# Output projection: every second weight tile's low half made by a negative on ScalarE and an adding transfer issued by GpSimd

## The chip, the cores and the metric

The kernel runs on one core of a Trainium2 chip. The metric is device time in microseconds of one execution; lower is better.

## What is computed

One layer of a streaming encoder, for 256 tokens of width 4096, all in 32-bit floats. It is cut here to what matters for the change, which lies in the last two lines but one:

```
proj = einsum('bsd,dc->bsc', x, w_in)              # one wide input projection
fox_out  = forgetting attention of some columns    # 16 heads of 128
rwkv_out = RWKV-7 scan of other columns            # 32 heads of 64
h    = concatenate([fox_out, rwkv_out], -1) * silu(z)
out  = einsum('bsc,cd->bsd', h, w_out)             # 4096 x 4096: the output projection
x    = layernorm(ALPHA * x + out, ln_gain, ln_bias)
```

## The kernel before

**Products in two halves.** TensorE's fast 32-bit format (F32R) keeps fewer bits than a float. So each operand is split into a high half, which is the value cast to F32R, and a low half, which is the value minus the high half. A product is then three matmuls into the same PSUM tile: high by high, low of the activations by high of the weights, and high of the activations by low of the weights. In the output projection these are the three lines of `project` (L882, L883, L884); L884 is the only one that reads the low half of the weights.

**The weight stream.** All weights are read once, in tiles of 128 partitions by 1024 values (512 KB), two steps of the contraction by 512 output columns. `stream` lists them in the order of use, first the input projection (names such as w3_1_7), then the output projection: `wo{b}_{q}` is tile q (0 to 15) of the block b (0 to 7) of 512 output columns. The profile leaves b out: all blocks' tiles 9 are wo_9, with wo_9h and wo_9l for their halves. Two functions keep the stream ahead of TensorE:

- `load` lets SP start the transfer of the next tile into one of four raw buffers (tag "wr").
- `fetch` takes the oldest raw tile and calls `split`: ScalarE casts it into one of four buffers for high halves (tag "wh", L141), VectorE subtracts the high half from the raw tile into one of three buffers for low halves (tag "wl", L142).

`weights(name)` is called ahead of each tile's matmuls and fetches until three tiles are ready. The order on each engine's queue comes from a scheduler, which starts from the order in which the program is written; an instruction waits on semaphores for what it reads and for the release of the buffer that it writes. A low half therefore waits for the last matmul that read the low half three tiles back, a high half for the last one that read the high half four tiles back, and a load for the last reader of the raw tile four back.

**The blocks.** Blocks 0 and 1 overlap with the end of the scan and with a change of memory pools. Blocks 2 to 7 run one after the other: for each of 16 tiles, two steps j and two halves m of the tokens, three matmuls each, 12 matmuls of 128x512 to a tile. After each block, VectorE adds the result to the residual and takes statistics (`add`, `gain`). In block 7, four tiles are held in buffers of their own (`kept`), and the second half of the tokens of the last tiles comes late, beside the layer norm.

Of the kernel before, what the change touches and what calls it, by code (L numbers as in the profile page):

```python
# [10 lines left out]
F32 = mybir.dt.float32  # L11
BF16 = mybir.dt.bfloat16
F32R = mybir.dt.float32r
AF = mybir.ActivationFunctionType
ALU = mybir.AluOpType
AX = mybir.AxisListType

P = 128
S = 256
D = 4096  # L20
KT = D // P
# [25 lines left out]
NB = D // OB  # L47
# [37 lines left out]
def layer(ctx: ExitStack, tc: tile.TileContext, xt, xtok, w_main, w_lora, w_first, muv, w_o, up, par, mulora, fbias, lng, lnb, cst, out):  # L85
    nc = tc.nc
# [5 lines left out]
    wpool = ctx.enter_context(tc.tile_pool(name="wpool", bufs=3))  # L92
# [20 lines left out]
    for n, (k0, k1) in enumerate(pieces):  # L113
        raw = spool.tile([P, 2 * S], F32, tag="xr", name=f"xr{n}", bufs=4)
        nc.sync.dma_start(out=raw[:, : (k1 - k0) * S], in_=xt[:, k0:k1, :].rearrange("p k t -> p (k t)"))
        x_raw.append(raw)
        raw = spool.tile([P, 2 * LA], F32, tag="lr", name=f"lr{n}", bufs=4)
        (nc.scalar if n < 3 else nc.sync).dma_start(out=raw[:, : (k1 - k0) * LA], in_=w_lora[:, k0:k1, :].rearrange("p k c -> p (k c)"))
        l_raw.append(raw)
        raw = wpool.tile([P, 1024], F32, tag="wr", name=f"wr{n}", bufs=4)  # L120
# [17 lines left out]
    def split(src, n, name, pool=wpool, tag="", cols=1024):  # L138
        hi = pool.tile([P, cols], F32R, tag="wh" + tag, name=name + "h", bufs=4 if pool is wpool else 1)
        lo = pool.tile([P, cols], F32R, tag="wl" + tag, name=name + "l")  # L140
        nc.scalar.copy(hi[:, :n], src[:, :n])  # L141
        latest[0] = nc.vector.tensor_tensor(lo[:, :n], src[:, :n], hi[:, :n].bitcast(F32), ALU.subtract)  # L142
        return hi, lo
# [14 lines left out]
    for n, (k0, k1) in enumerate(pieces):  # L158
# [6 lines left out]
        hi, lo = split(l_raw[n], (k1 - k0) * LA, f"wl{n}", spool, str(n % 3), 2 * LA)  # L165
        for j, m in steps(k1 - k0, False):
            mm(acc_l[m], m, k0 + j, hi, lo, j * LA, LA)
        hi, lo = split(w_raw[n], (k1 - k0) * LB, f"wr{n}")
# [38 lines left out]
    stream += [(f"wo{b}_{q}", w_o[b][:, 2 * q : 2 * q + 2, :]) for b, q in outs]  # L207
    stream.reverse()
    kept = {f"wo{NB - 1}_{KT // 2 - LATE + n}": n for n in range(LATE - 3)}
    rpool = None  # L210
    ready = []
    raws = []

    def load():
        if stream:
            name, src = stream.pop()
            raw = wpool.tile([P, 1024], F32, tag="wr", name=name, bufs=4)
            nc.sync.dma_start(out=raw, in_=src.rearrange("p k c -> p (k c)"))
            raws.append((name, raw))

    def fetch():
        while len(raws) < 3 and stream:
            load()
        if raws:
            name, raw = raws.pop(0)
            if name not in kept:
                ready.append((name, *split(raw, 1024, name)))
                return
            hl = []
            for j in range(4):  # L230
                hl.append(xpool.tile([P, OB], F32R, tag=f"x{4 * kept[name] + j}", name=f"{name}_{j}"))
            for j in range(2):
                r = raw[:, j * OB : (j + 1) * OB]
                nc.scalar.copy(hl[j], r)
                nc.vector.tensor_tensor(hl[2 + j], r, hl[j].bitcast(F32), ALU.subtract)
            ready.append((name, hl[:2], hl[2:]))

    def weights(name):
        while len(ready) < 3 and (stream or raws):
            fetch()  # L240
        got, hi, lo = ready.pop(0)
        assert got == name
        return hi, lo
# [704 lines left out]
    for b, q in outs:  # L948
        if q == 0:
            pool, tag = (ps, "ps") if b == 1 or b and b % 2 == 0 else (pp, "pp")  # L950
            oacc[b] = [pool.tile([P, 512], F32, tag=tag, name=f"oacc{b}_{m}") for m in range(2)]
        acc = oacc[b]
        hi, lo = weights(f"wo{b}_{q}")
        for j in range(2):
            k = 2 * q + j
# [46 lines left out]
    def moments(m):  # L1002
        mv = rpool.tile([P, 2], F32, name=f"mv{m}")
        sd = rpool.tile([P, 1], F32, name=f"sd{m}")
        rs = rpool.tile([P, 1], F32, name=f"rs{m}")
        s2 = rpool.tile([P, 1], F32, name=f"s2{m}")
        zh = rpool.tile([P, 1], F32R, name=f"zh{m}")
        z = factors(m, "d")
        nc.gpsimd.memset(z[:, 3:5], 1.0)
        za = factors(m, "a") if m else None  # L1010
        add(m, NB - 1)
        nc.vector.bn_aggr(mv, sums if m else st[m].rearrange("p b s -> p (b s)"))
        mean = mv[:, 0:1]
        nc.scalar.activation(sd, mv[:, 1:2], AF.Sqrt, bias=lneps)
        nc.vector.reciprocal(rs, sd)
        nc.vector.tensor_tensor(s2, mean, rs, ALU.mult)
        nc.vector.tensor_copy(zh, s2)
        nc.vector.tensor_copy(z[:, 0:3:2], zh.bitcast(F32).to_broadcast([P, 2]))
        last = nc.vector.tensor_tensor(z[:, 1:2], s2, zh.bitcast(F32), ALU.subtract)
        s2s.append(s2)  # L1020
        if m:
            for n, (v, at) in enumerate(((mean, (slice(0, 3, 2), slice(1, 2))), (sd, (slice(3, 5), slice(5, 6))))):
                h = rpool.tile([P, 1], F32R, name=f"zah{n}")
                nc.scalar.copy(h, v)
                nc.scalar.copy(za[:, at[0]], h.bitcast(F32).to_broadcast([P, 2]))
                nc.scalar.activation(za[:, at[1]], h.bitcast(F32), AF.Identity, scale=-1.0, bias=v)
        rss.append(rs)
        return z, za, last.ins
# [18 lines left out]
    z0, _, last = moments(0)  # L1047
# [26 lines left out]
    for n in range(HALVED):  # L1074
        b = HALVED + n
# [62 lines left out]
```

## Time and profile before

| | |
|---|---|
| median of 3 runs | 1917.95 us (1917.94 to 1918.83) |
| the profiled execution | 1917.13 us, its span 1915.3 us |
| TensorE busy | 1903.0 us, 99% of the span |
| VectorE, ScalarE, GpSimd busy | 1398.3, 985.9 and 261.5 us |
| granted TensorE clock, mean | 0.999 |
| blocks 2 to 6 of the output projection | about 1639 to 1859 us in the span |

PE stands for TensorE's matmuls, PEld for its weight loads, DVE for VectorE, ACT for ScalarE, POOL for GpSimd and SP for SyncE. The span goes from the first to the last instruction; the time of an execution has some 2 us more around it. A row of the timeline has the start and the duration in us, the engine, the line, the operation and what it writes and reads, and in brackets how long the engine had been idle before it and what ended that. Matmuls overlap: one is shown with 0.39 us, and the next starts about 0.23 us after it.

### The profile page before, as it was taken

The page shows a single profiled execution, that of the slowest core. Times are in us where ns is not written, and L with a number is a line of the kernel's source. Part 1 is how long each engine was busy: PE and PEld are TensorE (multiplying, and loading weights), DVE is VectorE, ACT ScalarE, POOL GpSimd, SP SyncE. Part 2 cuts the span into 40 slices and gives each one's busy share as a digit, 9 for nine tenths or more (in the row PEclk, how much of TensorE's full clock was granted, in tenths as well). Part 3 has the DMA queues.
Part 4 walks back from the last instruction along what each step waited for, and adds up shares of the span by engine and source line. Part 5 has one row for each costly group of instructions (what it writes and reads, how often), then busy time and mean ns, then how long its engine had stood idle before and what let it go on. Part 6 is the DMA issues. An engine that isn't in the chain of part 4 may idle for free.

```text
span 1915.3 us, 27998 instructions
## 1 busy us (share of the span) xinstructions
PE 1903.0 (99%) x9784; PEld 1584.8 (83%) x9784; DVE 1398.3 (73%) x2359; ACT 985.9 (51%) x1543; POOL 261.5 (14%) x463
## 2 busy tenths in 40 slices
PE   9999999999999999999999999999999999999998
PEld 9878888888888888888888888888888878888886
DVE  6677868786877687768776877787778865765555
ACT  6554565455545654465446554645464554444332
POOL 0022102110211021102200220022002201000000
PEclk9999999999999999999999999999999999999999
DMA  9578767876787677767876687668767976876664
GB/s 338 152 232 230 205 198 235 229 216 190 228 232 220 189 228 224 230 191 217 233 227 193 208 242 226 194 208 246 215 196 207 300 255 199 271 222 202 183 203 170
DMA packets 269682, 420.58 MB, mean 220 GB/s; under 512 B 142370, under 2 KB 169396, under 8 KB 269540
## 3 DMA queue, kind: packets, MB, share of 16 engines
q1 hardware_dynamic: 269108, 418.10, 72.8%
q8 instruction: 77, 1.26, 0.3%
q10 hardware_dynamic: 432, 0.69, 0.1%
q14 instruction: 65, 0.53, 0.1%
HBM read 389.07 MB, written 29.64 MB: 219 GB/s over the span
## 4 chain that ended last, share of the span: by engine, by line
PE 97%; DVE 1%; ACT 0%; issue 0%; DMA 0%; DVEq 0%; ACTq 0%
PE acc L147 24%; PE acc L149 24%; PE acc L148 24%; PE oacc L884 6%; PE oacc L882 6%; PE oacc L883 6%; PE rh L648 1%; PE gp L534 1%; PE up L679 1%; PE sp L689 1%; PE accl L147 1%; PE accl L148 1%; PE accl L149 1%; PE yp L711 0%; PE yp L709 0%; PE fsp L746 0%
## 5 line engine op out<-in xcount | busy, mean ns | idle before, releaser
L761 POOL COPY pT<-lg 32x96 f32<-32x96 f32 x128 | 58.5, 457 | 641.7 <-DVE lg L757 636.9
L604 DVE TENSOR_REDUCE xc<-prod 128x8 f32<-128x16 f32 (+30 forms) x248 | 72.7, 293 | 6.5
L571 POOL COPY BKt<-BK 32x192 f32<-32x192 f32 x128 | 68.6, 536 | 58.6 <-DVE BK L568 53.6
L601 DVE TENSOR_TENSOR prod<-Nb,xc 128x8 f32<-128x8 f32 (+30 forms) x248 | 72.2, 291 | 3.0
L142 DVE TENSOR_TENSOR w_0l<-w,w_0h 128x1024 fp32r<-128x1024 f32 x31 | 38.7, 1248 | 38.2 <-ACT w_0h L141 25.0
L141 ACT CAST w_0h<-w 128x1024 fp32r<-128x1024 f32 x31 | 32.5, 1048 | 51.5 <-DMA w<-in_w_main_dram 31.0
L142 DVE TENSOR_TENSOR w_11l<-w,w_11h 128x1024 fp32r<-128x1024 f32 x31 | 37.9, 1224 | 23.3 <-PE acc L149 17.7
L142 DVE TENSOR_TENSOR w_9l<-w,w_9h 128x1024 fp32r<-128x1024 f32 x31 | 38.0, 1225 | 21.6 <-issue 8.0
L142 DVE TENSOR_TENSOR w_10l<-w,w_10h 128x1024 fp32r<-128x1024 f32 x31 | 38.0, 1224 | 20.6 <-ACT w_10h L141 8.0
L142 DVE TENSOR_TENSOR w_15l<-w,w_15h 128x1024 fp32r<-128x1024 f32 x31 | 38.0, 1226 | 19.4 <-issue 15.9
L141 ACT CAST w_8h<-w 128x1024 fp32r<-128x1024 f32 x31 | 32.6, 1052 | 37.6 <-DMA w<-in_w_main_dram 12.5
L141 ACT CAST w_1h<-w 128x1024 fp32r<-128x1024 f32 x31 | 32.7, 1054 | 34.8 <-DMA w<-in_w_main_dram 18.9
L142 DVE TENSOR_TENSOR w_6l<-w,w_6h 128x1024 fp32r<-128x1024 f32 x31 | 37.9, 1221 | 17.3 <-ACT hry L722 10.3
L147 PE MATMUL acc<-w_15h,x 128*128 128x512 f32 x124 | 50.2, 405 | 0.0
L147 PE MATMUL acc<-w_9h,x 128*128 128x512 f32 x124 | 50.0, 403 | 0.0
L141 ACT CAST w_6h<-w 128x1024 fp32r<-128x1024 f32 x31 | 32.6, 1053 | 33.0 <-PE acc L148 23.0
L147 PE MATMUL acc<-w_14h,x 128*128 128x512 f32 x124 | 49.5, 399 | 0.0
L141 ACT CAST w_13h<-w 128x1024 fp32r<-128x1024 f32 x31 | 32.5, 1050 | 32.6 <-PE acc L148 31.9
L147 PE MATMUL acc<-w_1h,x 128*128 128x512 f32 x124 | 49.1, 396 | 0.0
L147 PE MATMUL acc<-w_2h,x 128*128 128x512 f32 x124 | 49.1, 396 | 0.0
L147 PE MATMUL acc<-w_0h,x 128*128 128x512 f32 x124 | 49.1, 396 | 0.0
L147 PE MATMUL acc<-w_5h,x 128*128 128x512 f32 x124 | 49.1, 396 | 0.0
(818 smaller groups left out, 6633.7 us busy)
## 6 DMA issues: line engine op xcount, KB each, us to landing
w<-in_w_main_dram SPq DMA_DIRECT2D x496, 512.0 KB, 4.1
wo<-in_w_o_dram SPq DMA_DIRECT2D x128, 512.0 KB, 4.1
bt<-bk SPq DMA_DIRECT2D x88, 128.0 KB, 4.2
Nb<-nd SPq DMA_DIRECT2D x16, 512.0 KB, 4.6
hd<-hl SPq DMA_DIRECT2D x29, 256.0 KB, 2.2
h<-hd SPq DMA_DIRECT2D x29, 256.0 KB, 6.1
wr<-in_w_first_dram SPq DMA_DIRECT2D x15, 384.0 KB, 6.1
lr<-in_w_lora_dram SPq DMA_DIRECT2D x14, 336.0 KB, 6.5
```

Source lines behind the costliest of these rows:

```text
L141: nc.scalar.copy(hi[:, :n], src[:, :n])
L142: latest[0] = nc.vector.tensor_tensor(lo[:, :n], src[:, :n], hi[:, :n].bitcast(F32), ALU.subtract)
L147: nc.tensor.matmul(acc[:, :n], xs[k][:, 0, tt], hi[:, o : o + n], start=(k == 0), stop=False)
L148: nc.tensor.matmul(acc[:, :n], xs[k][:, 1, tt], hi[:, o : o + n], start=False, stop=False)
L149: nc.tensor.matmul(acc[:, :n], xs[k][:, 0, tt], lo[:, o : o + n], start=False, stop=(k == KT - 1))
L571: nc.gpsimd.tensor_copy(BKt[B * b : B * (b + 1), :, :, B * a : B * (a + 1)], BK[B * a : B * (a + 1), :, : NCH - 1, B * b : B * (b + 1)])
L601: first = nc.vector.tensor_tensor(prod[:, :, :, s + 1 :], nb[:, :, s : s + 1, s + 1 :].to_broadcast([P, 2, NJ, w]), xc[:, :, :, s + 1 :], ...
L604: solved = nc.vector.tensor_reduce(xc[:, :, :, s : s + 1], prod[:, :, :, s:], AX.X, ALU.add)
L761: (nc.gpsimd.tensor_copy if b % 2 else nc.scalar.copy)(pT[B * b : B * (b + 1), :, B * a : B * (a + 1)], lg[B * a : B * (a + 1), :, B * b : ...
L882: nc.tensor.matmul(acc, ht[k][:, 0, tt], hi, start=(k == 0), stop=False)
L883: nc.tensor.matmul(acc, ht[k][:, 1, tt], hi, start=False, stop=False)
L884: nc.tensor.matmul(acc, ht[k][:, 0, tt], lo, start=False, stop=(k == KT - 1))
```

## The change

For the tiles 1, 3, 5, ... 15 of the blocks 2 to 6 (40 of the 80 tiles there) the low half is no longer a subtraction on VectorE. ScalarE casts the raw tile as before, then writes the negative of the high half into the low half's buffer, and GpSimd issues a transfer that reads the same weights from memory a second time and adds them to that buffer. The sum, weights minus high half, is the same low half. The buffers and their numbers stay as they are, and so do all the other tiles.

```diff
+    summed = {f"wo{b}_{q}" for b in range(2, NB - 1) for q in range(1, KT // 2, 2)}
...
-            raws.append((name, raw))
+            raws.append((name, raw, src))
...
-            name, raw = raws.pop(0)
+            name, raw, src = raws.pop(0)
+            if name in summed:
+                hi = wpool.tile([P, 1024], F32R, tag="wh", name=name + "h", bufs=4)
+                lo = wpool.tile([P, 1024], F32R, tag="wl", name=name + "l")
+                nc.scalar.copy(hi, raw)
+                nc.scalar.mul(lo, hi.bitcast(F32), -1.0)
+                nc.gpsimd.dma_start(out=lo, in_=src.rearrange("p k c -> p (k c)"), accum_op=ALU.add)
+                ready.append((name, hi, lo))
+                return
```

Nine lines are added ahead of most of the program, so that a line number after is larger by 9 for most rows: L884 of before is L893 after. The cast of a summed tile is L230, its negative L231, its transfer L232.

The scheduler places these as follows. On VectorE in block 3, tiles 8 to 12, before:

```order
L142 TENSOR_TENSOR wo_8l<-wo_8_16279,wo_8h 128x1024
L142 TENSOR_TENSOR wo_9l<-wo_9_16297,wo_9h 128x1024
L142 TENSOR_TENSOR wo_10l<-wo_10_16315,wo_10h 128x1024
L142 TENSOR_TENSOR wo_11l<-wo_11_16333,wo_11h 128x1024
L142 TENSOR_TENSOR wo_12l<-wo_12_16351,wo_12h 128x1024
```

After, with the statistics of the block before standing ahead of them:

```order
L142 TENSOR_TENSOR wo_4l<-wo_4_16204,wo_4h 128x1024
L142 TENSOR_TENSOR wo_6l<-wo_6_16241,wo_6h 128x1024
L882 TENSOR_SCALAR rt_17525<-rh_17523,cs 6x512
L883 SCALAR_TENSOR_TENSOR rows<-rr_17520,cs,rt_17525 6x512
L142 TENSOR_TENSOR wo_8l<-wo_8_16290,wo_8h 128x1024
L142 TENSOR_TENSOR wo_10l<-wo_10_16327,wo_10h 128x1024
L142 TENSOR_TENSOR wo_12l<-wo_12_16364,wo_12h 128x1024
```

The odd tiles' subtractions are gone and nothing has taken their place. ScalarE's queue at the same place, and GpSimd's, stand in the prediction. On TensorE four matmuls around the first tiles of blocks 2 to 4 change places with their neighbours; else its order is the same.

## The prediction

> **What bounds the kernel now.** I read the page first, for the busiest engine and for the chain of work that ended last.
>
> ```profile
> span 1915.3 us, 27998 instructions
> PE 1903.0 (99%) x9784; PEld 1584.8 (83%) x9784; DVE 1398.3 (73%) x2359; ACT 985.9 (51%) x1543; POOL 261.5 (14%) x463
> ...
> PE 97%; DVE 1%; ACT 0%; issue 0%; DMA 0%; DVEq 0%; ACTq 0%
> ```
>
> TensorE is busy for 99% of the span, and 97% of the chain is its matmuls. An average says little about one stage, so next the windows, one for each of the five blocks that the change touches.
>
> ```profile
> core 0: us, PE busy (x) PEld busy (x) DVE busy (x) ACT busy (x) POOL busy (x), PEclk, DMA share, GB/s
> 1639.00:1683.00 44.00, 43.97 (x194) 36.07 (x193) 30.50 (x35) 20.44 (x23) 0.00 (x0) 1.00 0.85 277
> ...
> 1771.00:1815.00 44.00, 44.00 (x195) 36.43 (x195) 23.67 (x24) 17.07 (x17) 0.00 (x0) 1.00 0.65 201
> 1815.00:1859.00 44.00, 44.00 (x195) 36.41 (x194) 23.66 (x24) 16.89 (x16) 0.00 (x0) 1.00 0.64 195
> sum 220.00, PE 219.97 PEld 181.79 DVE 128.50 ACT 91.12 POOL 0.00; mean PE 43.99 PEld 36.36 DVE 25.70 ACT 18.23 POOL 0.00
> ```
>
> TensorE is busy for 219.97 of 220.00 us at the full granted clock (1.00). VectorE, from which the change takes work, is busy for 128.50 us, ScalarE for 91.12 us, GpSimd not at all. The DMA engines are at 0.64 to 0.85 of their time. The waits of the weight loads into TensorE in 1640 to 1890 us have one row, and it is all that VectorE costs TensorE there.
>
> ```profile
> PEld oacc L884 <- DVE wo_2l L142: 0.5, 1, 0.5
> ```
>
> So a lighter VectorE is worth 0.5 us at most. What decides is whether the low half of a weight tile, made the new way, is still there when TensorE asks for it. The timeline of block 3 shows how early it is now. L882 and L883 multiply by the high half, L884 by the low half.
>
> ```profile
> 1699.40 1.05 ACT L141 CAST wo_9h<-wo 128x1024 fp32r<-128x1024 f32 x1 [1.10 <-PE oacc L883]
> ...
> 1701.92 0.39 PE L884 MATMUL oacc<-wo_6l,h 128*128 128x512 f32 x1
> ...
> 1702.12 1.06 ACT L141 CAST wo_10h<-wo 128x1024 fp32r<-128x1024 f32 x1 [1.67 <-PE oacc L883]
> 1702.15 0.39 PE L882 MATMUL oacc<-wo_7h,h 128*128 128x512 f32 x1
> ...
> 1702.41 1.23 DVE L142 TENSOR_TENSOR wo_9l<-wo,wo_9h 128x1024 fp32r<-128x1024 f32 x1 [1.55 <-PE oacc L884]
> ...
> 1704.87 0.39 PE L882 MATMUL oacc<-wo_8h,h 128*128 128x512 f32 x1
> ...
> 1707.59 0.39 PE L882 MATMUL oacc<-wo_9h,h 128*128 128x512 f32 x1
> ...
> 1707.82 0.19 PEld L884 LDWEIGHTS oacc<-wo_9l,h 128*128 128x128 f32 x1
> ```
>
> One tile takes TensorE 1704.87 - 1702.15 = 2.72 us. There are three buffers for low halves, so wo_9l can only be written when TensorE has let go of wo_6l: the subtraction starts at 1702.41, ends at 1703.64, and the first weight load that goes with wo_9l stands at 1707.82. That is 4.18 us in hand. A waiting matmul would hold up everything behind it on TensorE, whose queue is in order here.
>
> **Removed.** 40 of the 80 subtractions (8 in each of 5 blocks), 1.23 us each, 49 us of VectorE. TensorE never waited for them but in the row above, so they return between 0 and 0.5 us; I take 0. ScalarE's cast of the high half stays as it is. The raw tile of a summed name becomes free after that cast, not after the subtraction, so SP may send the load four tiles on a little sooner. No load is late now (the casts of block 3 above start on "PE oacc L883"), so that also gives nothing.
>
> **Added on ScalarE.** 40 negatives of 128x1024. The nearest row is its cast of the same shape, 1.06 us. With two casts to a pair of tiles that is 3 x 1.06 = 3.2 us in 5.44 us: ScalarE has the room. But the place in its queue counts. ScalarE in block 3, before:
>
> ```order
> L141 CAST wo_8h<-wo_8_16279 128x1024
> L141 CAST wo_9h<-wo_9_16297 128x1024
> L141 CAST wo_10h<-wo_10_16315 128x1024
> L141 CAST wo_11h<-wo_11_16333 128x1024
> L141 CAST wo_12h<-wo_12_16351 128x1024
> ```
>
> And the same place after (L230 is the cast of a summed tile, L231 the negative):
>
> ```order
> L141 CAST wo_8h<-wo_8_16290 128x1024
> L231 ACTIVATE wo_7l<-wo_7h 128x1024
> L230 CAST wo_9h<-wo_9_16308 128x1024
> L141 CAST wo_10h<-wo_10_16327 128x1024
> L231 ACTIVATE wo_9l<-wo_9h 128x1024
> L230 CAST wo_11h<-wo_11_16345 128x1024
> L141 CAST wo_12h<-wo_12_16364 128x1024
> ```
>
> All 40 negatives stand behind the cast of the next tile. That cast (wo_10h) waits for the end of wo_6h on TensorE, the same moment at which the buffer of wo_9l comes free. So the negative doesn't start at 1702.41 but after 1702.12 + 1.06 = 1703.18, and ends at about 1704.25 (1.06 again). From there to 1707.82 are 3.57 us, and the whole transfer has to fit in them: the hand-over to GpSimd, its issue, the data, the signal back.
>
> **Added on GpSimd and the DMA engines.** 40 transfers of 512 KB that read the weights once more and add them to what stands in the buffer. GpSimd's queue holds nothing else in these blocks:
>
> ```order
> L1018 MEMSET zd_17841 128x2
> L232 DMA wo_1l<-in_w_o_dram 128x1024
> L232 DMA wo_3l<-in_w_o_dram 128x1024
> L232 DMA wo_5l<-in_w_o_dram 128x1024
> L232 DMA wo_7l<-in_w_o_dram 128x1024
> ```
>
> So each waits for its negative alone, and who waits for it is TensorE at L893 (the L884 of before), with all its later matmuls. The trace of before has no transfer issued by GpSimd and none that adds. The nearest is the plain load of the same 512 KB by SP in the same stretch, from issue to landing:
>
> ```profile
> L218 SPq DMA_DIRECT2D wo<-in_w_o_dram x91: 327/328/335, 1640.3 to 1879.4; - x91
> ...
> DMA to landing us min/median/max: 3.6/3.8/4.4
> ```
>
> Call the time from the negative's end to the landing D. It costs nothing while D is under 3.57 us, and even the plain load's fastest is 3.6. The adding transfer has more to do: it reads the buffer too. One pass of 512 KB takes the engines 0.65 x 2.72 = 1.77 us (share of the windows by the time of a tile). In a full queue it is less: at the start of the kernel the engines moved 403 GB/s, which is 1.30 us for 512 KB.
>
> ```profile
> 12.00:16.00 4.00, 4.00 (x26) 4.00 (x26) 3.78 (x7) 3.53 (x8) 0.00 (x0) 1.00 1.04 403
> ```
>
> The third part is company. After the change the two loads of a pair come free nearly together (one by a cast, one by a subtraction), and the transfer meets their tail. How much a landing grows when loads come in a bunch is in the list of DMA issues by line (KB each, median us to landing):
>
> ```profile
> res<-in_xtok_dram SPq DMA_DIRECT2D x16, 256.0 KB, 5.1
> ...
> nb<-ncd SPq DMA_DIRECT2D x16, 128.0 KB, 8.7
> ...
> out_dram<-res SPq DMA_DIRECT2D x4, 512.0 KB, 2.6
> ```
>
> Loads of res, which leave in bunches, land after 5.1 us with half the bytes, 1.3 us over a lone weight load. I take D = 3.8 + 1.77 + 1.3 = 6.87 us. The bounds: the slowest plain load, 4.4, below, and above the slowest kind of landing in the trace with the second pass on it, 8.7 + 1.77 = 10.5. I stay nearer to the plain load, since rows of 4 KB are moved here and many short ones in nb. A row of this trace cannot say what the add itself costs.
>
> The Trainium skill (Collectives: The Full Stack, section "The bandwidth ceiling: the fold count and why AG ≠ RS ≠ AR") says the add costs no cycles of its own, but two source reads, which halve the rate. No run here shows it yet; with it alone, without company, D would be 3.8 + 1.77 = 5.57 and the kernel 40 us slower instead of 66.
>
> **The sum.** Let E = D - 3.57 = 3.30 us. The first summed tile stalls TensorE for E. That stall also lets the next one off, since the buffer of wo_11l (that of wo_8l) came free before the stall at wo_9l, and its transfer runs on meanwhile: two neighbouring summed tiles share one E between them. So 40 tiles cost 20 x E = 66 us. A second way gives the like: two loads and two passes to a pair, 4 x 1.77 = 7.1 us of the engines in 5.44 us, 1.6 over, times 40 is 66 us; by the 1.30 of the full queue they would just fit (5.2). The two are not added, since a stall of TensorE gives the engines the same time. The profiled execution took 1917.13 us with its span of 1915.3; 1917.13 + 66 = 1983. The median of the runs is 0.8 us above that execution, so 1984.
>
> **Rivals.** *The transfer is hidden, so not slower.* D stays under 3.76 us (E under 0.19, 3.8 us in all, 0.2% of the time, about what a measurement of this kernel can tell from no change); time 1918 to 1922. For it: stores of 512 KB land in 2.6 us. Against it: loads of 512 KB never landed under 3.6, and this one reads twice. Chance 0.05, and 0.08 more for the strip up to D = 4.4 (1922 to 1935). The Trainium skill (DMA: Bandwidth & Descriptors, section "Anatomy of one DMA — SWDGE (gpsimd) path") gives such a transfer 2.0 us plus its bytes over 436 GB/s, 3.2 us for 512 KB without an add; that would be this case, and the trace's 3.8 for a plain load speaks against it.
>
> *The clock drops.* Stalls of about 3.3 us come one at a time, and TensorE's clock may not outlast them. In the tail a wait of 1.26 us left it at 1.00; after the last matmul it fell.
>
> ```profile
> 1906.05 0.30 PE L1032 MATMUL zp<-cs,zd 128*128 128x128 f32 x1 [1.26 <-DVE zd L1019]
> ...
> 1908.21 0.40 PE L1082 MATMUL wp<-rows,la 128*128 128x512 f32 x1
> ```
>
> ```profile
> 1906.00:1910.00 4.00, 2.31 (x9) 1.49 (x9) 3.86 (x6) 2.86 (x6) 0.00 (x0) 1.00 0.43 160
> 1910.00:1915.00 5.00, 0.00 (x0) 0.00 (x0) 0.14 (x1) 0.00 (x0) 0.00 (x0) 0.67 0.77 295
> ```
>
> A mean of 0.67 over 5 us is half speed for 3.3 us, so the drop came at about 1911.7, 3.1 us after the last matmul. If every second summed tile had such a stall and the clock stayed down as long as the stall was, each would lose 1.65 us more, 33 us: 2017. It decides where stalls pass about 3.1 us and don't spread over two tiles. Chance 0.08. The Trainium skill (TensorE: Matmul & The Clock Gate, section "Part 1: The HAM clock gate (the "warmup" mystery)") has half rate after an idle window of about 3.4 us; the trace agrees with its 3.1.
>
> *The DMA engines become the bound.* If the add keeps them as long as four plain passes, 7.1 us, a pair needs 3.54 + 7.1 = 10.6 us instead of 5.44, the raw tiles come late too, and 40 pairs cost 207 us: 2124. It decides from about D = 10.5. Nothing here speaks for or against the rate of an adding transfer. Chance 0.12.
>
> That the low half isn't made as the change says is not a case of its own: the queues above show the instructions.
>
> **Numbers.** My case, D from 4.4 to 10.5 (17 to 139 us, 1935 to 2057), gets 0.67, with the likeliest at 1984. With the clock (0.08) and the lower end of the engine-bound case (some 0.04, up to 2065) the range 1935 to 2065 holds 0.79. Slower by over 0.2% are all cases but the hidden one. Faster has no mechanism beyond 0.5 us: 0.01. Same 0.05, slower 0.94.
>
> **What would show it.** Right: in the windows of blocks 2 to 6 TensorE's busy time per tile unchanged, but the five blocks 66 us longer; weight loads into TensorE at L893 waiting for the DMA of wo_1l, wo_3l and so on, some 3 us at every second of them or half that at each; the transfer landing near 6.9 us; block 7 as before. Wrong: no such waits (hidden); a granted clock under 1.00 in the blocks (clock); ScalarE's casts waiting for raw tiles and a DMA share near 1 (engine-bound).

## The result, and the profile after

The changed kernel takes 1994.58 us (1991.32 to 1997.17) against 1917.95 us before, a ratio of 1.0401 (95% interval 1.0388 to 1.0414): 76.6 us slower, where 66 us were forecast. The profiled execution's span is 1991.7 us, 76.4 us more than before. The page of the changed kernel shows the DMA queue of the loads (q1) and the new one of the adding transfers (q0), each with its packets, its MB and its share of the 16 engines' time, and the chain of work that ended last:

```profile
q1 hardware_dynamic: 269108, 418.10, 68.9%
q0 software_dynamic: 5760, 20.97, 6.2%
...
PE 81%; issue 13%; DVE 2%; POOL 2%; DMA 1%; ACT 1%; SPq 0%; POOLq 0%; DVEq 0%; ACTq 0%
```

TensorE's share of the chain falls from 97% to 81%. That is no measure of the loss: 16% of the span would be some 320 us. It says that the chain now also runs over other engines. The windows of the changed kernel in the same stretch as before show where TensorE loses time:

```profile
core 0: us, PE busy (x) PEld busy (x) DVE busy (x) ACT busy (x) POOL busy (x), PEclk, DMA share, GB/s
1639.00:1683.00 44.00, 32.39 (x127) 25.49 (x126) 15.42 (x20) 19.24 (x21) 5.36 (x6) 0.88 0.89 256
...
1727.00:1771.00 44.00, 38.59 (x164) 29.85 (x163) 13.70 (x16) 21.72 (x23) 5.30 (x7) 1.00 0.86 230
1771.00:1815.00 44.00, 37.63 (x156) 29.70 (x155) 8.49 (x7) 19.42 (x19) 5.93 (x7) 0.96 0.88 232
1815.00:1859.00 44.00, 37.67 (x143) 29.47 (x142) 10.43 (x13) 18.14 (x18) 5.17 (x6) 0.88 0.82 219
```

Where TensorE was busy for all of 44 us, it is now for 32 to 39 us, and the granted clock, 1.00 before, is down to 0.88 in two of these windows: two losses, not one. VectorE's relief (over the whole kernel its busy time falls from 1398.3 to 1348.1 us) shows up nowhere in the time. The waits of TensorE's weight loads in the changed kernel (us in total, how many, the longest):

```profile
PEld oacc L893 <- DMA wo_3l<-in_w_o_dram: 13.9, 4, 5.2
PEld oacc L893 <- DMA wo_1l<-in_w_o_dram: 10.7, 4, 7.7
PEld oacc L893 <- DMA wo_15l<-in_w_o_dram: 10.4, 5, 4.0
PEld oacc L893 <- DMA wo_11l<-in_w_o_dram: 9.7, 5, 2.4
PEld oacc L893 <- DMA wo_7l<-in_w_o_dram: 9.0, 4, 2.3
PEld oacc L893 <- DMA wo_13l<-in_w_o_dram: 4.2, 5, 1.5
PEld oacc L893 <- DMA wo_9l<-in_w_o_dram: 3.1, 2, 2.1
PEld oacc L893 <- DMA wo_5l<-in_w_o_dram: 3.1, 1, 3.1
```

The unevenness is what sharing would look like: 3, 7, 11 and 15 pay 43.0 of the 64.1 us, their neighbours less; of the 10.7 us at tile 1, 7.7 are one wait at the start of block 2. One such tile on the timeline, from the negative (ScalarE) over the issue (GpSimd) to the standstill of TensorE:

```profile
1784.29 1.05 ACT L141 CAST wo_8h<-wo 128x1024 fp32r<-128x1024 f32 x1 [1.71 <-PE oacc L892]
1785.24 1.06 ACT L231 ACTIVATE wo_7l<-wo_7h 128x1024 fp32r<-128x1024 f32 x1
...
1786.59 0.86 POOL L232 DMA_DIRECT2D wo_7l<-in_w_o_dram  x1 [8.82 <-ACT wo_7l L231]
...
1789.98 0.39 PE L892 MATMUL oacc<-wo_7h,h 128*128 128x512 f32 x1
1792.24 0.50 PE L893 MATMUL oacc<-wo_7l,h 128*128 128x512 f32 x1 [1.87 <-DMA wo_7l<-in_w_o_dram]
```

The negative ends at 1786.30, GpSimd starts 0.29 us later and needs 0.86 us to issue, and TensorE goes on at 1792.24: D, taken up to there, is 5.94 us. Up to the landing itself it is 5.96 us in the median of the 40 tiles and 6.6 in the mean. All 40 transfers, from the start of GpSimd's instruction to the landing:

```profile
DMA to landing us min/median/max: 5.3/5.7/9.9
```

I worked TensorE's loss out from the starts of its matmuls in 1636 to 1950 us: a distance before a matmul that waited for a DMA, less the 0.227 us of an undisturbed one, is a wait; other distances over 0.3 us are slow matmuls. The changed kernel has 27 waits with 55.9 us, 18.7 us of them in block 2, and 97 slow matmuls that cost 17.2 us. (The rows of the weight loads add up to more, 64.1 us, because a weight load runs ahead of its matmul and so begins to wait sooner.) Most of the slow ones come in runs behind waits, at a distance of 0.43 us instead of 0.227:

```profile
1832.92 0.80 PE L893 MATMUL oacc<-wo_3l,h 128*128 128x512 f32 x1 [3.14 <-DMA wo_3l<-in_w_o_dram]
1833.51 0.63 PE L891 MATMUL oacc<-wo_3h,h 128*128 128x512 f32 x1
1833.94 0.63 PE L892 MATMUL oacc<-wo_3h,h 128*128 128x512 f32 x1
1834.37 0.63 PE L893 MATMUL oacc<-wo_3l,h 128*128 128x512 f32 x1
```

Together these are 73 of the 76 us. The other 3 I did not trace.

The trace's own record of the granted clock, of which PEclk is the mean, shows where these runs come from. In blocks 2 to 6 it has eight spells of half clock, each 3.41 or 6.83 us long, and all of them start on one grid of 3.41 us. 14.0 of the 17.2 us of slow matmuls lie in these spells; most of the rest is 0.11 us right behind each wait. Each spell began behind a step of the grid in which TensorE had waited for 1.97 us or more, and no step with 1.90 us or less was followed by one. (In e2 below the border is not as sharp: with 1.93 to 1.98 us of waiting in a step, spells follow some and not others.)

### The profile page after: what moved, and what is told of

It reads as the page before. It is cut to its first block, busy times and chain, and to the rows that moved or that the text cites. A ratio compares the mean times of both kernels' runs of the same rounds, so it can differ in the third digit from the quotient of the medians.

```text
span 1991.7 us, 28059 instructions
## 1 busy us (share of the span) xinstructions
PE 1924.9 (97%) x9784; PEld 1590.6 (80%) x9784; DVE 1348.1 (68%) x2319; ACT 1023.9 (51%) x1583; POOL 299.8 (15%) x503
## 4 chain that ended last, share of the span: by engine, by line
PE 81%; issue 13%; DVE 2%; POOL 2%; DMA 1%; ACT 1%; SPq 0%; POOLq 0%; DVEq 0%; ACTq 0%
PE acc L147 23%; PE acc L149 23%; PE acc L148 23%; PE oacc L893 2%; PE oacc L891 2%; PE oacc L892 2%; PE rh L657 1%; PE gp L543 1%; DMA wo<-in_w_o_dram 1%; PE up L688 1%; PE sp L698 1%; PE accl L149 0%; PE accl L148 0%; PE accl L147 0%; PE yp L720 0%
## 5 line engine op out<-in xcount | busy, mean ns | idle before, releaser
L580 POOL COPY BKt<-BK 32x192 f32<-32x192 f32 x128 | 72.9, 569 | 58.6 <-DVE BK L577 53.6
L149 PE MATMUL acc<-w_5l,x 128*128 128x512 f32 x124 | 48.5, 391 | 1.5 <-DVE w_5l L142 1.5
```

Source lines behind the costliest of these rows:

```text
L149: nc.tensor.matmul(acc[:, :n], xs[k][:, 0, tt], lo[:, o : o + n], start=False, stop=(k == KT - 1))
L580: nc.gpsimd.tensor_copy(BKt[B * b : B * (b + 1), :, :, B * a : B * (a + 1)], BK[B * a : B * (a + 1), :, : NCH - 1, B * b : B * (b + 1)])
```

## The experiments

Theory: the transfer comes late by E after the release of its buffer, two neighbouring summed tiles share one E, and long waits drop the clock. Rival: the DMA engines' time per pair of tiles is the bound. "Waits" and "slow" below are worked out as above, from one profiled execution each.

**e1, the negative ahead of the next cast.**

```diff
+    negs = []
...
-                nc.scalar.mul(lo, hi.bitcast(F32), -1.0)
+                negs.append(nc.scalar.mul(lo, hi.bitcast(F32), -1.0))
...
-                ready.append((name, *split(raw, 1024, name)))
+                with tc.issue_after(negs.pop().ins) if negs else ExitStack():
+                    ready.append((name, *split(raw, 1024, name)))
```

> The negative stands ahead of the next tile's cast on ScalarE, so it ends 1.06 us sooner after the release of its buffer; nothing else changes. Latency theory (the transfer is late by E after the release of the buffer, two neighbouring summed tiles share one E): E falls by 1.06, the waits of TensorE for the transfer by 20 x 1.06 = 21 us, and with fewer long waits some 10 us of half-rate matmuls go too: about 1958 to 1974. Rival (the DMA engines' time per pair of tiles is the bound): the same bytes by the same engines, 1990 to 1997 as before.

Measured 1980.63 us (ratio 1.0323, 1.0303 to 1.0342): 14 us back, too little for the first theory and too much for the rival. Waits 46.1, slow 15.5. The landing of this kernel's transfers tells why:

```profile
DMA to landing us min/median/max: 5.4/6.3/9.3
```

Half of the 1.06 us won was lost again to a median landing 0.6 us later.

**e2, every fourth tile.**

```diff
-    summed = {f"wo{b}_{q}" for b in range(2, NB - 1) for q in range(1, KT // 2, 2)}
+    summed = {f"wo{b}_{q}" for b in range(2, NB - 1) for q in range(1, KT // 2, 4)}
```

> Only tiles 1, 5, 9 and 13 of blocks 2 to 6 are made the new way, 20 instead of 40. Latency theory with sharing: a summed tile no longer has a stalled neighbour, so each bears its own E; 20 x E as with 40 tiles, so the loss stays at three quarters to the whole of 76 us: 1975 to 1995. Rival (a price per transfer, of engine time or of issue): half the loss, 1950 to 1958.

Measured 1984.48 us (ratio 1.0338, 1.0314 to 1.0362). Half the transfers cost 67 of the 77 us, so no price per transfer explains the loss. In the waits of TensorE's weight loads each of the four tiles of each block now waits, every time:

```profile
PEld oacc L893 <- DMA wo_1l<-in_w_o_dram: 15.8, 5, 6.7
PEld oacc L893 <- DMA wo_9l<-in_w_o_dram: 12.6, 5, 3.7
PEld oacc L893 <- DMA wo_13l<-in_w_o_dram: 12.0, 5, 3.1
PEld oacc L893 <- DMA wo_5l<-in_w_o_dram: 11.1, 5, 2.9
```

20 waits, 46.2 us, and 19.0 us slow. The transfers landed no later than in the changed kernel (5.5 us in the median against 5.7), so it is not a longer transfer that made each tile dearer. The sharing is shown.

**e3, no add.**

```diff
-                nc.gpsimd.dma_start(out=lo, in_=src.rearrange("p k c -> p (k c)"), accum_op=ALU.add)
+                nc.gpsimd.dma_start(out=lo, in_=src.rearrange("p k c -> p (k c)"))
```

> The same transfers by GpSimd over the same bytes, written over the negative and not added (the low half is then the whole weight: the add is what is left out). If the second pass over the buffer is what makes the transfer longer than a plain load, it lands 1 to 1.8 us sooner, waits fall by 20 to 36 us, and the time is 1940 to 1970. Rival (GpSimd's way of issuing is the whole price and the add is free): 1985 to 1997, the landing at 5.5 to 5.9 us as with the add.

Measured 1956.51 us (ratio 1.0198, 1.0181 to 1.0215), half the loss. GpSimd's issue shortens from 0.86 to 0.53 us, and the landing:

```profile
DMA to landing us min/median/max: 3.8/4.6/8.4
```

1.1 us sooner. The add is about half of the price; the other half is that there is a second transfer behind a negative at all.

**e4, no transfer.**

```diff
-                nc.gpsimd.dma_start(out=lo, in_=src.rearrange("p k c -> p (k c)"), accum_op=ALU.add)
+                nc.vector.tensor_tensor(lo, raw, lo.bitcast(F32), ALU.add)
```

> ScalarE makes the negative at the same place as in the changed kernel, and VectorE adds the raw tile to it; there is no second transfer. Latency theory: 1.06 + 1.23 us of work end some 2.3 us ahead of TensorE's need, so 1917 to 1920, the time of before. Rival (the longer ScalarE queue and the chain of the two engines cost by themselves): 1925 or more.

Measured 1919.04 us (ratio 1.0003, 0.9993 to 1.0012): no difference. ScalarE's longer queue costs nothing by itself.

**e5, the low half's products last.** In a summed tile TensorE does the eight products with the high half first and the four with the low half after them (`first_two` holds the first two lines of `project`, `third` the last):

```diff
...
+                if f"wo{b}_{q}" in summed:
+                    first_two(acc[m], k, j, m, hi)
+                    if j and m:
+                        for jj in range(2):
+                            for mm_ in range(2):
+                                third(acc[mm_], 2 * q + jj, jj, mm_, lo)
...
```

> In the summed tiles the four products with the low half come after the eight with the high half, so the low half is wanted 6 matmuls or 1.36 us later; the transfers are untouched. Latency theory: E falls by 1.36, the waits by 20 x 1.36 = 27 us and most of the half-rate matmuls (about 10 us) with them: 1950 to 1968. Rival (engine time): 1990 to 1997.

Measured 1972.44 us (ratio 1.0277, 1.0258 to 1.0297), 4 us above the range. Waits 41.2, slow 8.9; landing 6.4 us in the median. Again time in hand helps, and again part of it goes to a later landing.

**e6, both.** The edits of e1 and e5.

> Both: the negative ahead of the next cast, and the products with the low half last; 1.06 + 1.36 = 2.42 us more in hand. Latency theory: outside block 2, where two waits of neighbouring tiles add up to 1.9 to 2.1 us now, no wait is left; block 2 keeps some: 1920 to 1940. Rival (engine time, 41.5% of it by the adding queue): above 1960.

Measured 1959.36 us (ratio 1.0212, 1.0183 to 1.0241): 19 us above the first theory's range and 0.6 us under the rival's bound, so the time alone doesn't speak against the rival. Waits 25.4, slow 11.8; landing 6.4 us.

**e7, nobody waits.**

```diff
+                aside = rpool.tile([P, 768], F32R, tag="as", name=name + "s", bufs=2)
...
-                nc.scalar.mul(lo, hi.bitcast(F32), -1.0)
-                nc.gpsimd.dma_start(out=lo, in_=src.rearrange("p k c -> p (k c)"), accum_op=ALU.add)
+                nc.scalar.mul(aside, hi[:, :768].bitcast(F32), -1.0)
+                nc.vector.tensor_tensor(lo, raw, hi.bitcast(F32), ALU.subtract)
+                nc.gpsimd.dma_start(out=aside, in_=src.rearrange("p k c -> p (k c)")[:, :768], accum_op=ALU.add)
```

> VectorE makes all low halves again as in the kernel before, and beside that ScalarE writes negatives of three quarters of each summed tile (128x768) into a tile that nobody reads, to which GpSimd's transfers add the same three quarters of the weights: the DMA engines' extra work without anybody waiting for it. Latency theory: 1917 to 1922. Rival (crowding: the loads of raw tiles get late beside adding transfers): 1930 to 1970.

Measured 1922.98 us (ratio 1.0026, 1.0016 to 1.0036), just above the first theory's range. Of the 5 us, TensorE's weight loads spent 3.8 waiting for low halves from VectorE; no more of it is traced. The DMA engines are full and TensorE still runs without a break, as this kernel's window shows (share in the last column but one):

```profile
1771.00:1815.00 44.00, 44.00 (x196) 36.43 (x195) 23.18 (x22) 23.94 (x25) 7.38 (x9) 1.00 0.98 272
```

So full engines and late loads cost these 5 us at most. But the landing of its smaller transfers, beside loads at full pace, is long:

```profile
DMA to landing us min/median/max: 5.1/7.6/9.0
```

**e8, four low buffers.**

```diff
-                lo = wpool.tile([P, 1024], F32R, tag="wl", name=name + "l")
+                own_lo = int(name.split("_")[1]) % 4 == 1
+                lo = (rpool if own_lo else wpool).tile([P, 1024], F32R, tag="wl", name=name + "l", bufs=1 if own_lo else 3)
```

and the edit of e1.

> One more buffer for low halves (tiles 1, 5, 9 and 13 of blocks 2 to 6 use it), so every low half waits for the release four tiles back instead of three, 2.72 us sooner; the negative stands ahead of the next cast. Latency theory: 2.72 + 1.06 - what is lost as the negative now follows its own cast, about 2.7 us more in hand, more than the E of 1.9 to 2.1 outside block 2: 1918 to 1930. Rival (engine time): above 1960.

Measured 1954.01 us (ratio 1.0184, 1.0157 to 1.0210). Outside both ranges. In this window of the kernel the granted clock is whole and the engines are nearly full, and the landing is long:

```profile
1771.00:1815.00 44.00, 40.56 (x172) 31.32 (x171) 12.35 (x13) 22.56 (x22) 6.04 (x7) 1.00 0.95 255
```

```profile
DMA to landing us min/median/max: 6.0/7.8/9.2
```

Waits 28.0, slow 6.7. The less TensorE waits, the more loads run beside the transfer and the later it lands: 5.7, 6.3, 6.4, 7.8 us in the changed kernel, e1, e5 and e8. In the traces the loads' queue moved 134, 152, 171 and 200 KB per us in these four while an adding transfer was under way. That the company causes the late landing is argued from this order, not shown by a run of its own. My theory had taken the landing as fixed. Two readings were left for the 36 us: full engines, or the later landing by itself.

**e9, every fourth tile with four buffers.** The edits of e2 and e8.

> Tiles 1, 5, 9 and 13 of blocks 2 to 6 only, with the fourth buffer for low halves and the negative ahead of the next cast. Engine-time theory for what is left with four buffers (two loads of 1.65 us and one adding transfer of 3.1 us make 6.4 us in 5.44 us of a pair): with one adding transfer in four tiles it is 4 x 1.65 + 3.1 = 9.7 us in 10.9 us, so the engines keep up: 1917 to 1926, the upper end for block 2, where other loads crowd. Rival (a late landing of 7 to 8 us goes on costing each summed tile about 1 us): 1935 to 1945.

Measured 1947.31 us (ratio 1.0162, 1.0144 to 1.0180): the rival, 2 us above its range. The engines are at 0.81 in its window, yet TensorE waits about 1.2 us at most summed tiles:

```profile
1771.00:1815.00 44.00, 41.48 (x179) 33.39 (x180) 15.89 (x17) 19.11 (x19) 3.45 (x4) 1.00 0.81 221
```

```profile
wo_5l<-in_w_o_dram POOLq DMA_DIRECT2D x4, 512.0 KB, 7.3
wo_9l<-in_w_o_dram POOLq DMA_DIRECT2D x4, 512.0 KB, 6.6
```

The landing is 7.4 us in the median: it can be as late where the engines are not full. How many loads run beside the transfer doesn't explain it alone, as the loads' queue moved 163 KB per us here, less than in e5, where the transfers landed after 6.4.

**e10, four buffers and no add.** The edits of e8 and e3.

> Four buffers, negative first, all 40 transfers, but written over the negative instead of added (the add is left out, so the low half is the whole weight). Engine-time theory: 2 x 1.65 + 1.84 = 5.1 us in 5.44 us, so it fits outside block 2: 1918 to 1930. Rival (GpSimd's transfers cost by their way of issue and not by the second pass): 1940 to 1955 as with the add.

Measured 1925.65 us (ratio 1.0044, 1.0027 to 1.0061), 28 us under e8. Without the second pass the transfers fit nearly everywhere but in block 2.

**e11, filled waits.** Every fourth tile as in e2, and ahead of its first product:

```diff
+FILL = 8
...
+                if f"wo{b}_{q}" in summed and not j and not m:
+                    fill = pst(f"fill{b}_{q}")
+                    for _ in range(FILL):
+                        nc.tensor.matmul(fill, ht[k][:, 0, :P], hi[:, :OB], start=True, stop=True)
```

> Every fourth tile as in e2, and 8 matmuls ahead of each summed tile whose result nobody reads: 8 x 0.227 = 1.8 us of work inside a wait of about 2 us or more. Clock theory (the waits drop the granted clock, and 17 to 19 us of the loss are matmuls at half rate): waits get shorter by what the added matmuls take, TensorE's standstills stay under 1.5 us outside block 2, and 10 to 19 us come back: 1965 to 1975. Rival (the slow matmuls have another cause): 1980 to 1990, or more by what the 8 matmuls add.

Measured 1972.30 us (ratio 1.0290, 1.0273 to 1.0307): 12 us faster than e2 with 160 matmuls more. The granted clock over the span goes from 0.990 to 0.998 and the slow matmuls from 19.0 to 6.3 us. The added matmuls take 160 x 0.227 = 36.3 us and 9.8 us of waits are left, together what the waits alone were in e2; so the 12 us are the clock's. The lost clock is shown to be a cost of its own, and the standstill its cause.

**e12, every fourth tile, four buffers, low half last.** The edits of e9 and e5.

> As e9 (every fourth tile, fourth buffer, negative first), with the products with the low half last, so that it is wanted 1.36 us later. In e9 the transfers landed after 6.5 to 7.6 us, and TensorE stood 1.2 us before each summed tile. Crowded-landing theory (beside loads at full pace an adding transfer lands some 2 us later than in the pauses of a waiting TensorE, and only the time in hand counts): 1.36 us more covers it outside block 2, 1920 to 1928. Rival (something in each summed tile costs TensorE by itself, such as the queue of the transfers): 1940 to 1947 as in e9.

Measured 1927.17 us (ratio 1.0049, 1.0032 to 1.0066), 20 us under e9 with the same 20 transfers, which landed no sooner (7.6 us in the median against 7.4): time in hand was what was missing. No variant is faster than the kernel before.

## Why the prediction was right

*Nothing to gain.* As forecast: VectorE was busy for 50 us less and nothing came back. e4, with the transfer taken out, is the time of before, so the negatives cost nothing either.

*The place in ScalarE's queue.* The negative behind the next cast was read from the order; e1 shows it costs 14 us, not the 21 that 1.06 us times 20 makes.

*The length of the transfer.* D was put at 6.87 us from a plain load, a second pass and a crowd; it measured 5.96 in the median, up to 10.2 in block 2. The time in hand was put at 3.57 us; where no stall went ahead it was 3.91. The second pass was put at 1.77 us; with the add the landing is 1.1 us longer (the changed kernel against e3). By queue, the adding transfers take 41.5% of the engines in 1639 to 1935 us, 0.415 x 296 / 40 = 3.1 us each, against the 3.54 taken for two passes and 1.8 us each without the add in e3.

```profile
q1 hardware_dynamic: 14530, 47.97, 45.2%
q0 software_dynamic: 5760, 20.97, 41.5%
```

*Two tiles share one E.* Shown by e2, and by the changed kernel's own trace: in block 4 wo_7l had 3.91 us in hand, took 5.90 and stalled TensorE for 2.03; wo_9l behind it then had 6.08 us in hand, took 5.76 and cost nothing. In blocks 3 to 6 two neighbours' waits add up to 2.3 us in the mean, mostly about 2, where 3.30 was forecast; block 2, where other loads crowd, has 18.7 us in eight tiles.

*Whether the wait is the right one.* For each summed tile the traces give the time in hand and D. What D exceeds it by, added up over the tiles, is 55.0 us in the changed kernel, 45.4 in e2, 27.9 in e8 and 23.7 in e9, within 2 us of the waits of each. So the mechanism of the forecast holds in all of them. What it had wrong is a D that stays as it is when more time is given to it.

*The sum.* The step that was mis-sized is E: 66 us of waits were forecast, 55.9 came. The total came near (1984 forecast, 1994.58 measured) because a term that stood among the rivals, the clock, came on top with 17.2 us (33 were its price there). That the two misses offset each other is luck: the waits alone would have made 1974. The forecast and that rival were not exclusive, and I had treated them so. The threshold was wrong too: read from the tail as 3.1 us, while runs of slow matmuls followed waits of 2.65 and 2.8 us, and in two places one of 2.0. Other waits of 2.0 and 2.1 us had none behind them; those two lay whole within one step of the clock's grid, and the others were split by it. The trace so does not bear out the 3.4 us that the Trainium skill (TensorE: Matmul & The Clock Gate, section "Part 1: The HAM clock gate (the "warmup" mystery)") gives for an idle window as the length that a single wait must have. A slip without weight: the chances of the cases add up to 1.00 without the 0.01 for faster, so slower has 0.95 by them and not 0.94.

*Hidden.* Against it the prediction had the plain load's 3.6 us, and no transfer landed under 5.3. The 3.2 us that the Trainium skill gives (DMA: Bandwidth & Descriptors, section "Anatomy of one DMA — SWDGE (gpsimd) path") are for a transfer without an add; e3's fastest took 3.8, counted from the start of GpSimd's instruction, which takes 0.53 of it.

*Engines as the bound.* Not in the changed kernel (share 0.82 to 0.89, and e2 with half the transfers costs nearly as much). In e8 the waits and the slow matmuls are 34.7 of the 36 us, and the waits are those of its own late transfers. How much of that lateness comes from full engines stays open.

## What to carry to other kernels

A buffer that passes through one more hand (a transfer instead of an operation on the spot) has to be ready in the time between its release and its next use: count that time from the rotation and the queue order before counting bytes or busy shares. With few buffers a late producer's price need not fall with the number of late tiles, since neighbours can share one delay; here halving the work bought 10 us of 77. And a landing that is measured while the consumer stands still is too short a price for a kernel in which it doesn't.

## What the runs showed of the hardware

An adding transfer of 512 KB issued by GpSimd took 0.86 us to issue (0.53 without the add) and landed after 5.7 us in the median, 1.1 us later than the same transfer without the add. It occupied the DMA engines for 3.1 us. Landing stretched to 7.8 us in the median of e8, where TensorE, and with it the loads, ran nearly at full pace; the issue stayed at 0.86 us. TensorE's matmuls ran at half rate, 0.43 us apart instead of 0.227, in runs of 7 to 14 behind waits. The spells of half clock lasted 3.41 or 6.83 us and started on one grid of 3.41 us; in the changed kernel they followed the steps with at least 1.97 us of waiting and none with 1.90 or less. Filling the waits with matmuls brought 12.7 of 19.0 us of slow matmuls back.
